# High weights meet high and low activations in one 512-column matmul

## The chip, the cores and the metric

One core of a Trainium2 chip runs the whole computation in one launch. The metric is the device time of that launch in microseconds (us). Before the change it is 994.75 us, the median of three runs from 994.37 to 995.06.

## The reference

The computation is one transformer layer followed by a second block of two, on 256 tokens of width 1024, all in float32. Only the matrix products and what follows them matter here:

```python
# first block
p = rmsnorm(x, g_attn) @ w_in                     # then two gated convolutions and stick-breaking attention
x = x + mixed @ w_out
x = x + square(relu(rmsnorm(x, g_ffn) @ w_ff1)) @ w_ff2
# second block, layer 0: retention; layer 1: differential attention over shared K and V
q, k, v, g = split(rms_norm(x, g) @ a_w_in)       # q and k are then rotated (cos, sin)
h = (silu(g) * rms_norm(retention(q, k, v))) @ a_w_out
kv = rms_norm(x, kv_norm) @ w_kv;  q = rms_norm(x, g) @ b_w_q
# after each of them
h = rms_norm(x, g) @ w_up                         # 2 x 2816 columns
hc = conv_b + sum(shift(h, 2 - j) * conv_w[j] for j in range(3))
h = (silu(hc[gate half]) * hc[up half]) @ w_down
```

## The kernel before

Every float32 operand of a large product is split in two parts that TensorE takes in its faster float32 form: high = the rounded value, low = the value minus high. A product is then three matmuls, high x high, high x low and low x high, added up in one PSUM bank. Weights come from memory packed in units of 128x1024 values; `loader` fetches two units at a time, `splitter` (`split_one`, L369) makes the high part on ScalarE (a copy) and the low part on VectorE (a subtraction) into a ring of eight units.

A unit is used in one of three ways. In `xstat_mm` and `down_mm` the activations are stationary and the weights move past them, 512 columns at a time. In `wstat` (L508) the weights are stationary: a unit is eight tiles of 128x128 and 256 tokens move past each, so that the result has channels on partitions and tokens along the row. For each of the eight tiles (a k step) it issues the three matmuls, 24 in a block, each of 256 columns, and `yield`s between steps. There are 142 such blocks: 14 in the mixing stage, 24 in the feed-forward stage (`ff_phase`), 16 in retention (`ret_phase`, four per head), 36 in each of the two convolution stages (`conv_phase`, a gate block and an up block per step) and 16 in the differential attention (`diff_phase`, two per head). The result of a block is 256 columns, half a bank; in retention and in the convolution stages two blocks share one bank.

The activations are held by `Acts` (L239): a high tile and a low tile of 8 x 256 values per partition, each allocated on its own. `sx` serves all stages, `sb` the queries of the differential attention.

What follows a block: `evac` of `ff_phase` (ScalarE relu out of the bank, VectorE square, `split_to`, which makes the high and low part for the down product); `rotate` (two VectorE products of the bank with cosine and sine, then a difference and a sum); `gate` (two `conv`s, each one ScalarE operation and two on VectorE that read the bank, then silu, a product and `split_to`); `evac` of `diff_phase` (one ScalarE copy).

The down products run behind the up blocks: `lagged` puts the down step of unit i five steps after its up step. `Down` holds four PSUM banks as accumulators (two for each half of the tokens). For the last seven units (TAIL) it does the first half of the tokens first, then hands that half to the chain of norms that leads to the next stage, and does the second half meanwhile.

The order of all instructions is fixed when the kernel is built, by a small simulation (`Flow`): each engine has a queue ordered by priority (CHAIN, ATT, EVAC, SPLIT, IDLE, MAIN), each operation has a cost in ns, and `Slots` stand for buffers: a process that asks for more than is free waits in line. `banks` are the eight PSUM banks, `cvs` three pairs of convolution buffers, `rots` one set of rotation buffers. On the chip each engine works off its list in that order and waits for semaphores. Every operation is recorded with the line L198, where the simulation issues it, so groups are told apart by the names of tiles: `hi`, `lo` are weights, `xh`, `xl` activations, `fh`, `fl` the inputs of a down product, `cv` convolution results.

Of the kernel before, what the change touches and what calls it, by code (L numbers as in the profile page):

```python
# [18 lines left out]
P = 128  # L19
# [219 lines left out]
class Acts:  # L239


    def __init__(self, hi, lo):
        self.hi, self.lo = hi, lo
        self.reset()

    def reset(self):
# [11 lines left out]
def chain_kernel(ctx: ExitStack, tc: tile.TileContext, x_in, wpack, gains, chan, small_rows, consts, out):  # L258
# [151 lines left out]
    mhalf = cpool.tile([P, 4], F32, tag="mhalf", name="mhalf")  # L410
    nc.gpsimd.memset(mhalf, -0.5)
    ch = cpool.tile([P, NCH], F32, tag="ch", name="ch")
    sx = Acts(cpool.tile([P, KD, S], F32R, tag="xh", name="xh"), cpool.tile([P, KD, S], F32R, tag="xl", name="xl"))

    junk = cpool.tile([P, 512], BF16, tag="junk", name="junk")

# [68 lines left out]
    def residual_post(t, acc, ready, g, hg):  # L485
# [19 lines left out]
        banks.put(2)  # L505
        return [stt(p, x, h, r, x, ALU.mult, ALU.add) for x, h in zip(xs, hs)]

    def wstat(dst, w, sx):  # L508
        hi, lo = yield from take("ws", w)
        h3 = hi.rearrange("p (k c) -> p k c", k=KD)  # L510
        l3 = lo.rearrange("p (k c) -> p k c", k=KD)
        for k in range(KD):
            if k % 4 == 0:
                yield sx.ready[0][k // 4]
                yield sx.ready[1][k // 4]
            o = pe(MAIN, 358, [
                mm(dst, h3[:, k, :], sx.hi[:, k, :], k == 0, False),
                mm(dst, h3[:, k, :], sx.lo[:, k, :], False, False),
                mm(dst, l3[:, k, :], sx.hi[:, k, :], False, k == KD - 1)])
            yield o.end  # L520
        release(ring, o)
        return o
# [377 lines left out]
    def ff_phase(fp):  # L900
        w1, w2 = "w_ff1", "w_ff2"
        fhs = slots(fp, TAIL + 2, [P, S], F32R, "fh")
        fls = slots(fp, TAIL + 2, [P, S], F32R, "fl")
        rls = slots(fp, 2, [P, S], F32, "rl")
        both = Slots(flow, TAIL + 2, lambda: (fhs.make(), fls.make()))
        ys = {}
        f8 = [fp.tile([P, 8, S], F32R, tag=f"f8{c}", name=f"f8{c}") for c in "hl"]
        nat = fp.tile([P, 2, D], F32, tag="nat", name="nat")
        r8 = [[Ev(), Ev()], [Ev(), Ev()]]

        def nat_evac_of(c):
            cs = slice(c * 512, c * 512 + 512)
            ks = slice(4 * c, 4 * c + 4)

            def nat_evac(t, d, o):
                yield o
                n = nat[:, t, cs]
                yield act(EVAC, n, d, AF.Relu)
                banks.put()
                yield tt(EVAC, n, n, n, ALU.mult)  # L920
                pt = yield from banks.get()
                yield tp(EVAC, [(pt[:, j * P:(j + 1) * P], n[:, j * P:(j + 1) * P]) for j in range(4)])
                tsl = slice(t * P, (t + 1) * P)
                yield from split_to(EVAC, f8[0][:, ks, tsl], f8[1][:, ks, tsl], pt.rearrange("p (k c) -> p k c", k=4))
                banks.put()
                flow.fire(r8[c][t])
            return nat_evac

        yield from xstat_tokens(w1, sx, [nat_evac_of(0), nat_evac_of(1)])
        for i in range(8):  # L930
            ys[i] = ((f8[0][:, i, :], f8[1][:, i, :]), flow.spawn(both_of(r8[i // 4])), None)

        def evac(pp, o, y):
            yield o
            rl = yield from rls.get()
            yield act(EVAC, rl, pp[:, :S], AF.Relu)
            banks.put()
            yield tt(EVAC, rl, rl, rl, ALU.mult)
            yield from split_to(EVAC, y[0], y[1], rl)
            rls.put()  # L940

        preload(AF.Silu)
        g_final = yield from load_gain(G_FINAL)
        a_pre = yield from load_gain(A_PRE)

        def chain(t, acc, o):
            xs = yield from big.get()
            ops = yield from residual_add(t, acc, o)
            r = yield from rstd_halves(CHAIN + 0.1 * t, halves(x_t[t]), ops)
            g, gop = g_final  # L950
            yield gop
            ops = [stt(CHAIN + 0.1 * t, xh_, xh_, r, g_, ALU.mult, ALU.mult) for xh_, g_ in zip(halves(x_t[t]), halves(g))]
            yield from prenorm(t, xs, [(a_pre, sx)], ops)
            big.put(3 if t == 1 else 1)

        dn = Down(w2, NF, chain, sx)
        for what, i in lagged(NF, 8):
            if what == "up":
                pp = yield from banks.get()
                o = yield from wstat(pp[:, :S], w1, sx)  # L960
                y = yield from both.get()
                ys[i] = (y, flow.spawn(evac(pp, o, y)), both)
            else:
                yield from dn.step(*ys.pop(i))
# [8 lines left out]
    def ret_phase(rp):  # L973
# [7 lines left out]
        o_ready = [[Ev(), Ev()] for _ in range(RH)]  # L981
        vs = Slots(flow, 1, lambda: [rp.tile([P, 2, 512], F32R, tag=f"v{c}", name=nm("v")) for c in "hl"])
        qs = [Slots(flow, 1, lambda w=w: rp.tile([P, 2, S], F32, tag=f"q{w}", name=nm("q"))) for w in range(2)]
        rots = Slots(flow, 1, lambda: [rp.tile([P, 2, S], F32, tag=f"rot{c}", name=nm("rot")) for c in "cs"])
        pds = Slots(flow, 1, lambda: [rp.tile([P, 384], d, tag=f"pd{c}", name=nm("pd")) for c, d in (("f", F32), ("h", F32R), ("l", F32R))])
        sgs = slots(rp, 2, [P, 512], F32, "sgl")

        def rotate(pp, o, dst):
            yield o
            for c in cops:  # L990
                yield c
            tcos, tsin = yield from rots.get()
            p3 = pp.rearrange("p (a c) -> p a c", a=2)
            a = tt(EVAC, tcos, p3, cosb.broadcast_to([P, 2, S]), ALU.mult)
            b = tt(EVAC, tsin, p3, sinb.broadcast_to([P, 2, S]), ALU.mult)
            yield a
            yield b
            banks.put()
            a = tt(EVAC, dst[:, 0, :], tcos[:, 0, :], tsin[:, 1, :], ALU.subtract)
            b = tt(EVAC, dst[:, 1, :], tsin[:, 0, :], tcos[:, 1, :], ALU.add)  # L1000
            yield a
            yield b
            rots.put()
# [60 lines left out]
        for h in range(RH):  # L1064
# [28 lines left out]
                f_pre = yield from load_gain(F0_PRE)  # L1093
            pr = []
            for what in range(2):
                pp = yield from banks.get()
                yield from wstat(pp[:, 0:S], "a_w_in_2", sx)
                o = yield from wstat(pp[:, S:2 * S], "a_w_in_2", sx)
                d = yield from qs[what].get()
                pr.append((d, flow.spawn(rotate(pp, o, d))))  # L1100
            pd_ev = flow.spawn(scores(h, pr[0][0], pr[1][0], pr[0][1], pr[1][1], box, dec, dop))
# [10 lines left out]
    def conv_phase(layer, fp, gain_ids, chain_of):  # L1112
# [2 lines left out]
        fls = slots(fp, TAIL + 2, [P, S], F32R, "fl")  # L1115
        both = Slots(flow, TAIL + 2, lambda: (fhs.make(), fls.make()))
        cvs = Slots(flow, 3, lambda: [fp.tile([P, S], F32, tag=f"cv{c}", name=nm("cv"), bufs=3) for c in range(2)])
        nat = fp.tile([P, 2, D], F32, tag="nat", name="nat")
        n_ready = [[Ev(), Ev()], [Ev(), Ev()]]

# [6 lines left out]

        def gate(pp, o_g, o_u, i, y, nat_i):
            cg, cu = yield from cvs.get()
            ps_g, ps_u = pp[:, 0:S], pp[:, S:2 * S]  # L1130
            if nat_i is not None:
                for e in n_ready[0] + n_ready[1]:
                    yield e
                o_g, o_u = [tp(EVAC, [(d[:, t * P:(t + 1) * P], nat[:, t, c0 + nat_i * P:c0 + (nat_i + 1) * P]) for t in range(2)])
                            for d, c0 in ((ps_g, 0), (ps_u, 512))]
            yield o_g
            yield o_u
            a = flow.spawn(conv(EVAC, ps_g, cg, 0, i))
            b = flow.spawn(conv(EVAC, ps_u, cu, 1, i))
            yield a  # L1140
            o = act(EVAC, cg, cg, AF.Silu)
            yield b
            banks.put()
            yield o
            yield tt(EVAC, cg, cg, cu, ALU.mult)
            yield from split_to(EVAC, y[0], y[1], cg)
# [23 lines left out]
            ys[i] = (y, flow.spawn(early(i, y)), both)  # L1170
        for what, i in lagged(NF2, 4):
            if what == "up":
                pp = yield from banks.get()
                o_g = yield from wstat(pp[:, 0:S], w_up, sx)
                o_u = yield from wstat(pp[:, S:2 * S], w_up, sx)
                y = yield from both.get()
                ys[i] = (y, flow.spawn(gate(pp, o_g, o_u, i, y, None)), both)
            else:
                yield from dn.step(*ys.pop(i))

    def diff_phase(dp, sb):
# [24 lines left out]
        aas = slots(dp, 2, [P, 384], F32, "aT")  # L1206
        o1s = slots(dp, 2, [P, 2, P], F32, "o1")

        def evac(pp, o, d, p):
            yield o  # L1210
            yield act(p, d, pp[:, :S], AF.Copy)
            banks.put()

        def head(h, p, q, k, qr, kr, v, v_in):
# [100 lines left out]
        for h in range(DH):  # L1315
            pr = []
            p = CHAIN + 0.5 if h >= DH - URGENT else ATT
            for what in range(2):
                pp = yield from banks.get()
                o = yield from wstat(pp[:, :S], "w_kv_2" if what == 0 else "b_w_q_2", sx if what == 0 else sb)  # L1320
                d = yield from qks[what].get()
                pr.append((d, flow.spawn(evac(pp, o, d, p if h >= DH - URGENT else EVAC))))
            heads.append(flow.spawn(head(h, p, pr[1][0], pr[0][0], pr[1][1], pr[0][1], v, v_in)))

        def coarse():
# [17 lines left out]
    def main():  # L1343
# [4 lines left out]
        with tc.tile_pool(name="retp", bufs=1, reuse_waits="tile") as rp:  # L1348
            yield from ret_phase(rp)
        with tc.tile_pool(name="bresp", bufs=1, reuse_waits="tile") as bp:  # L1350
            sb = Acts(bp.tile([P, KD, S], F32R, tag="bh", name="bh"), bp.tile([P, KD, S], F32R, tag="bl", name="bl"))
            with tc.tile_pool(name="cf0p", bufs=1, reuse_waits="tile") as fp:
                yield from conv_phase(0, fp, (F0_POST, KV_G, B_PRE), lambda f_post, kv_g, b_pre: (
                    lambda t, acc, o: chain_post(t, acc, o, f_post, [(kv_g, sx), (b_pre, sb)])))
# [103 lines left out]
```

## Time and profile before

| | |
|---|---|
| median of three runs | 994.75 us |
| profiled execution | 995.56 us |
| its span (first to last instruction) | 993.8 us |
| TensorE (PE) busy | 980.7 us, 99% |
| weight loads (PEld) busy | 876.1 us, 88% |
| VectorE (DVE) busy | 689.3 us, 69% |
| ScalarE (ACT) busy | 562.5 us, 57% |
| GpSimd (POOL) busy | 30.2 us, 3% |
| read from memory | 178.08 MB |

The span is what the profile sees of the execution; 1.76 us lie around it. Busy is the union of the times in which at least one instruction of the engine was under way. Matmuls overlap each other, and their ends are modelled, so for PE one reads the starts. A time in a row of the timeline is counted from the start of the span.

### The profile page before, as it was taken

How to read it: one execution, taken by the hardware profiler on the slowest of the kernel's cores; microseconds unless marked ns; L12 is line 12 of the kernel's file. 1: busy time of each engine (PE TensorE's matmuls, PEld its weight loads, DVE VectorE, ACT ScalarE, POOL GpSimd, SP SyncE). 2: the span in 40 equal slices, each digit the busy share in tenths (PEclk: the TensorE clock that was granted, in tenths of full speed). 3: DMA queues.
4: the chain of work that ended last, by engine and by line, in shares of the span. 5: the costliest groups of instructions: out<-in, count | busy, mean ns of one | idle time of the engine just before them, and what ended most of it. 6: DMA issues, size and time to landing. Idle time of an engine off the chain costs nothing.

```text
span 993.8 us, 15342 instructions
## 1 busy us (share of the span) xinstructions
PE 980.7 (99%) x6108; PEld 876.1 (88%) x6108; DVE 689.3 (69%) x1076; ACT 562.5 (57%) x952; POOL 30.2 (3%) x52
## 2 busy tenths in 40 slices
PE   7999999999999999999999999999999999999997
PEld 5899889999988989988889999997899789999996
DVE  5899775555558756665579666668777579776663
ACT  6654564444446444544567555556677767555551
POOL 1000000000000000000000000001000100000000
PEclk9999999999999999999999999999999999999999
DMA  8744455555436744554366555543733155655531
GB/s 300 257 133 176 179 212 187 195 173 207 171 128 228 264 164 147 178 188 174 123 219 250 185 192 173 209 169 135 266 148 134 54 199 205 236 182 177 184 107 43
DMA packets 28585, 180.14 MB, mean 181 GB/s; under 512 B 3168, under 2 KB 4448, under 8 KB 8672
## 3 DMA queue, kind: packets, MB, share of 16 engines
q1 hardware_dynamic: 28512, 179.14, 50.7%
q8 instruction: 48, 0.79, 0.3%
q14 instruction: 25, 0.20, 0.1%
HBM read 178.08 MB, written 1.05 MB: 180 GB/s over the span
## 4 chain that ended last, share of the span: by engine, by line
PE 92%; DVE 2%; ACT 2%; issue 2%; DMA 1%; POOL 1%; SPq 0%; DVEq 0%; POOLq 0%; ACTq 0%
PE bank L198 92%; ACT junk L198 1%; DVE lo L198 1%; DMA big<-gains 1%; POOL tiny L198 1%; DVE x L198 1%; DVE big L198 0%; ACT hi L198 0%; ACT L198 0%; DVE tiny L198 0%; ACT pe L198 0%; ACT aT L198 0%; DVE xl L198 0%; ACT dyh L198 0%; SPq L198 0%
## 5 line engine op out<-in xcount | busy, mean ns | idle before, releaser
L198 DVE TENSOR_TENSOR lo<-raw,hi 128x1024 fp32r<-128x1024 f32 (+1 forms) x344 | 393.7, 1153 | 129.7 <-ACT hi L198 128.5
L198 ACT ACTIVATE hi<-raw 128x1024 fp32r<-128x1024 f32 (+1 forms) x344 | 341.2, 1003 | 154.6 <-PE bank L198 138.9
L198 PE MATMUL bank<-xh,hi 128*128 128x256 f32 x1072 | 306.1, 286 | 0.0
L198 PE MATMUL bank<-xh,lo 128*128 128x256 f32 x1072 | 303.3, 283 | 0.0
L198 PE MATMUL bank<-xl,hi 128*128 128x256 f32 x1072 | 303.3, 283 | 0.0
L198 PEld LDWEIGHTS bank<-xh,hi 128*128 128x128 f32 x1072 | 205.4, 192 | 3.7 <-issue 1.0
L198 PEld LDWEIGHTS bank<-xl,hi 128*128 128x128 f32 x1072 | 205.4, 192 | 2.6
L198 PEld LDWEIGHTS bank<-xh,lo 128*128 128x128 f32 x1072 | 205.3, 191 | 0.0
L198 PE MATMUL bank<-hi,xh 128*128 128x512 f32 x288 | 114.1, 396 | 0.0
L198 PE MATMUL bank<-lo,xh 128*128 128x512 f32 x288 | 112.4, 390 | 0.2 <-DVE lo L198 0.2
L198 PE MATMUL bank<-hi,xl 128*128 128x512 f32 x288 | 112.5, 391 | 0.0
L198 DVE SCALAR_TENSOR_TENSOR cv<-bank,ch,cv 128x254 f32<-128x254 f32 (+1 forms) x176 | 72.5, 476 | 51.6 <-ACT cv L198 51.4
L198 PE MATMUL bank<-hi,fh 128*128 128x512 f32 x272 | 106.9, 393 | 0.0
L198 PE MATMUL bank<-lo,fh 128*128 128x512 f32 x272 | 106.5, 391 | 0.0
L198 PE MATMUL bank<-hi,fl 128*128 128x512 f32 x272 | 105.8, 389 | 0.0
L198 ACT ACTIVATE cv<-bank,ch 128x256 f32<-128x256 f32 x88 | 44.1, 561 | 61.4 <-PE bank L198 61.4
L198 PEld LDWEIGHTS bank<-hi,xl 128*128 128x128 f32 x288 | 54.0, 188 | 11.8 <-DVE xl L198 0.2
L198 PEld LDWEIGHTS bank<-lo,xh 128*128 128x128 f32 x288 | 54.2, 188 | 11.5 <-DVE lo L198 1.0
L198 PEld LDWEIGHTS bank<-hi,xh 128*128 128x128 f32 x288 | 54.1, 188 | 10.4
L198 PEld LDWEIGHTS bank<-hi,fl 128*128 128x128 f32 x272 | 51.1, 188 | 11.0
L198 PEld LDWEIGHTS bank<-hi,fh 128*128 128x128 f32 x272 | 51.3, 189 | 9.1
L198 PEld LDWEIGHTS bank<-lo,fh 128*128 128x128 f32 x272 | 51.3, 189 | 8.5
(167 smaller groups left out, 1039.8 us busy)
## 6 DMA issues: line engine op xcount, KB each, us to landing
raw<-wpack SPq DMA_DIRECT2D x155, 1024.0 KB, 4.8
big<-gains SPq DMA_DIRECT2D x12, 512.0 KB, 6.9
raw<-wpack SPq DMA_DIRECT2D x12, 512.0 KB, 6.9
x<-x SPq DMA_DIRECT2D x4, 256.0 KB, 6.1
out_dram<-x SPq DMA_DIRECT2D x4, 256.0 KB, 2.2
dec<-consts SPq DMA_DIRECT2D x4, 192.0 KB, 5.0
one<-consts SPq DMA_DIRECT2D x1, 384.0 KB, 6.3
ch<-chan SPq DMA_DIRECT2D x1, 213.5 KB, 5.9
```

The source lines that it names most:

```text
L198: fn(*a, **k)
```

## The change

In 124 of the 142 weight-stationary blocks the high weights meet high and low activations in one matmul. For that the two parts of the activations stand in one tile, and the moving operand of the first matmul is the view `both[:, :, k, :]`, two strips of 256 columns. Its result is 512 columns, a whole bank: high x high in the first half, high x low in the second. The low weights meet the high activations in a second matmul of 256 columns, which is added to the second half. After the block the two halves are added: `join` copies the second half out of the bank on ScalarE and adds the first on VectorE. The mixing stage and heads 6 and 7 of the differential attention keep three matmuls. Retention and the convolution stages take two banks per pair of blocks in place of one, and `gate` and `rotate` read the joined sums from new buffers (`sums`, two pairs; a third buffer in `rots`). The planner's cost of a k step is 352 (merged) and 360 (not merged), where it was 358.

```diff
 class Acts:
-    def __init__(self, hi, lo):
-        self.hi, self.lo = hi, lo
+    def __init__(self, both):
+        self.both = both
+        self.hi, self.lo = both[:, 0], both[:, 1]
         self.reset()
...
-    sx = Acts(cpool.tile([P, KD, S], F32R, tag="xh", name="xh"), cpool.tile([P, KD, S], F32R, tag="xl", name="xl"))
+    sx = Acts(cpool.tile([P, 2, KD, S], F32R, tag="xhl", name="xhl"))
...
+    def join(p, out, d):
+        yield act(p, out, d[:, S:], AF.Copy)
+        yield tt(p, out, d[:, :S], out, ALU.add)
+
     def wstat(dst, w, sx):
...
+        merged = dst.shape[-1] == 2 * S
         for k in range(KD):
...
-            o = pe(MAIN, 358, [
-                mm(dst, h3[:, k, :], sx.hi[:, k, :], k == 0, False),
-                mm(dst, h3[:, k, :], sx.lo[:, k, :], False, False),
-                mm(dst, l3[:, k, :], sx.hi[:, k, :], False, k == KD - 1)])
+            if merged:
+                o = pe(MAIN, 352, [
+                    mm(dst.rearrange("p (a c) -> p a c", a=2), h3[:, k, :], sx.both[:, :, k, :], k == 0, False),
+                    mm(dst[:, S:], l3[:, k, :], sx.hi[:, k, :], False, k == KD - 1)])
+            else:
+                o = pe(MAIN, 360, [
+                    mm(dst, h3[:, k, :], sx.hi[:, k, :], k == 0, False),
+                    mm(dst, h3[:, k, :], sx.lo[:, k, :], False, False),
+                    mm(dst, l3[:, k, :], sx.hi[:, k, :], False, k == KD - 1)])
...
         def evac(pp, o, y):                       # feed-forward
             yield o
             rl = yield from rls.get()
-            yield act(EVAC, rl, pp[:, :S], AF.Relu)
+            yield from join(EVAC, rl, pp)
             banks.put()
-            yield tt(EVAC, rl, rl, rl, ALU.mult)
+            yield stt(EVAC, rl, rl, 0.0, rl, ALU.max, ALU.mult)
...
-            tcos, tsin = yield from rots.get()
-            p3 = pp.rearrange("p (a c) -> p a c", a=2)
+            tcos, tsin, p3 = yield from rots.get()
+            for j in [flow.spawn(join(EVAC, p3[:, n, :], pp[n])) for n in range(2)]:
+                yield j
+            banks.put(2)
...
-                pp = yield from banks.get()
-                yield from wstat(pp[:, 0:S], "a_w_in_2", sx)
-                o = yield from wstat(pp[:, S:2 * S], "a_w_in_2", sx)
+                pp = yield from banks.get(2)
+                yield from wstat(pp[0], "a_w_in_2", sx)
+                o = yield from wstat(pp[1], "a_w_in_2", sx)
...
+        sums = Slots(flow, 2, lambda: [fp.tile([P, S], F32, tag=f"sum{c}", name=nm("sum"), bufs=2) for c in range(2)])
...
         def gate(pp, o_g, o_u, i, y, nat_i):
             cg, cu = yield from cvs.get()
...
+            else:
+                ps_g, ps_u = yield from sums.get()
+                yield o_g
+                yield from join(EVAC, ps_g, pp[0])
+                banks.put()
+                yield o_u
+                yield from join(EVAC, ps_u, pp[1])
+                banks.put()
...
-                pp = yield from banks.get()
-                o_g = yield from wstat(pp[:, 0:S], w_up, sx)
-                o_u = yield from wstat(pp[:, S:2 * S], w_up, sx)
+                pp = yield from banks.get(2)
+                o_g = yield from wstat(pp[0], w_up, sx)
+                o_u = yield from wstat(pp[1], w_up, sx)
...
+                merged = h < DH - 2
+                o = yield from wstat(pp if merged else pp[:, :S], "w_kv_2" if what == 0 else "b_w_q_2", sx if what == 0 else sb)
```

## Rows read from the trace of the kernel before

**Rows 1.** The page, its first part: engines' busy us, share of span, instructions.
```profile
PE 980.7 (99%) x6108; PEld 876.1 (88%) x6108; DVE 689.3 (69%) x1076; ACT 562.5 (57%) x952; POOL 30.2 (3%) x52
```

**Rows 2.** The page's chain of work that ended last, shares of the span.
```profile
PE 92%; DVE 2%; ACT 2%; issue 2%; DMA 1%; POOL 1%; SPq 0%; DVEq 0%; POOLq 0%; ACTq 0%
```

**Rows 3.** The view of waits, PE alone: total us, times, longest.
```profile
PE bank L198 <- DVE big L198: 3.2, 3, 2.6
...
```

**Rows 4.** Timeline of PE, 149.6 to 157.3 us: start, us, what.
```profile
149.64 0.39 PE L198 MATMUL bank<-hi,f8h 128*128 128x512 f32 x1
...
154.40 0.28 PE L198 MATMUL bank<-xh,hi 128*128 128x256 f32 x1
...
154.63 0.28 PE L198 MATMUL bank<-xh,lo 128*128 128x256 f32 x1
...
157.27 0.40 PE L198 MATMUL bank<-hi,f8h 128*128 128x512 f32 x1
```

**Rows 5.** Groups by form, PE: count, busy us, mean ns, idle before.
```profile
L198 PE MATMUL bank<-xh,hi 128*128 128x256 f32 x1072 | 306.1, 286 | 0.0
...
L198 PE MATMUL bank<-bh,hi 128*128 128x256 f32 x64 | 18.3, 286 | 0.0
```

**Rows 6.** Groups by form and timeline of PE, the mask matmul.
```profile
L198 PE MATMUL bank<-trib,identb 128*128 128x256 bf16 x8 | 1.6, 278 | 0.0
...
42.83 0.39 PE L198 MATMUL bank<-trib,identb 128*128 128x256 bf16 x2
```

**Rows 7.** Groups by form of ACT and of DVE.
```profile
L198 ACT ACTIVATE q<-bank 128x256 f32<-128x256 f32 x16 | 6.3, 395 | 5.4 <-PE bank L198 5.4
L198 ACT ACTIVATE junk<-x 128x512 bf16<-128x512 f32 x28 | 17.6, 629 | 16.9 <-DVE x L198 14.8 <-DMA x<-x 1.6
L198 ACT ACTIVATE junk<-bank 128x512 bf16<-128x512 f32 x24 | 14.3, 596 | 26.4 <-PE bank L198 25.9
...
L198 DVE TENSOR_TENSOR bank<-bank,tri 128x256 f32<-128x256 f32 x16 | 6.8, 425 | 2.1 <-PE bank L198 2.0
...
L198 DVE SCALAR_TENSOR_TENSOR cb<-gpad,ch,cb 128x256 f32<-128x256 f32 x60 | 25.5, 474 | 0.0
L198 DVE SCALAR_TENSOR_TENSOR cv<-bank,ch,cv 128x255 f32<-128x255 f32 x88 | 38.5, 478 | 51.6 <-ACT cv L198 51.4
```

**Rows 8.** Windows: us, busy us of PE, PEld, DVE, ACT, POOL; clock; DMA.
```profile
202.50:259.00 56.50, 56.50 (x363) 51.53 (x362) 32.13 (x40) 27.26 (x42) 0.00 (x0) 1.00 0.53 189
...
567.50:652.50 85.00, 85.00 (x602) 80.09 (x602) 58.17 (x91) 48.41 (x71) 0.00 (x0) 1.00 0.53 186
...
709.40:771.20 61.80, 61.55 (x507) 57.27 (x507) 44.68 (x113) 46.08 (x138) 4.15 (x6) 1.00 0.49 181
```

**Rows 9.** Windows of 5 us, start of the first convolution stage.
```profile
522.50:527.50 5.00, 5.00 (x44) 5.00 (x44) 5.00 (x13) 3.41 (x7) 0.00 (x0) 1.00 1.03 432
...
537.50:542.50 5.00, 5.00 (x33) 4.51 (x32) 5.00 (x9) 2.66 (x7) 0.00 (x0) 1.00 0.60 218
```

**Rows 10.** Timeline of DVE and of PE at that start.
```profile
520.44 4.13 DVE L198 SCALAR_TENSOR_TENSOR cv<-bank,ch,cv 128x255 f32<-128x255 f32 x10
...
527.06 0.42 DVE L198 TENSOR_TENSOR fl<-cv,fh 128x256 fp32r<-128x256 f32 x1
...
530.67 3.99 DVE L198 SCALAR_TENSOR_TENSOR cv<-bank,ch,cv 128x255 f32<-128x255 f32 x10
...
533.32 0.28 PE L198 MATMUL bank<-xh,hi 128*128 128x256 f32 x1
```

**Rows 11.** Timeline of ACT, DVE and PE, end of the first convolution stage.
```profile
665.41 1.02 ACT L198 ACTIVATE cv<-bank,ch 128x256 f32<-128x256 f32 x2 [1.57 <-PE bank L198]
...
668.03 1.22 DVE L198 TENSOR_TENSOR lo<-raw,hi 128x1024 fp32r<-128x1024 f32 x1
...
670.07 0.42 DVE L198 TENSOR_TENSOR fl<-cv,fh 128x256 fp32r<-128x256 f32 x1 [0.48 <-ACT fh L198]
...
672.49 0.39 PE L198 MATMUL bank<-hi,fl 128*128 128x512 f32 x1
```

More of the change, by code (lines that the diff above doesn't have):

```diff
@@ L959, in ff_phase @@
                 pp = yield from banks.get()
-                o = yield from wstat(pp[:, :S], w1, sx)
+                o = yield from wstat(pp, w1, sx)
                 y = yield from both.get()
@@ L983, in ret_phase @@
         qs = [Slots(flow, 1, lambda w=w: rp.tile([P, 2, S], F32, tag=f"q{w}", name=nm("q"))) for w in range(2)]
-        rots = Slots(flow, 1, lambda: [rp.tile([P, 2, S], F32, tag=f"rot{c}", name=nm("rot")) for c in "cs"])
+        rots = Slots(flow, 1, lambda: [rp.tile([P, 2, S], F32, tag=f"rot{c}", name=nm("rot")) for c in "csq"])
         pds = Slots(flow, 1, lambda: [rp.tile([P, 384], d, tag=f"pd{c}", name=nm("pd")) for c, d in (("f", F32), ("h", F32R), ("l", F32R))])
@@ L997, in rotate @@
             yield b
-            banks.put()
             a = tt(EVAC, dst[:, 0, :], tcos[:, 0, :], tsin[:, 1, :], ALU.subtract)
@@ L1129, in gate @@
             cg, cu = yield from cvs.get()
-            ps_g, ps_u = pp[:, 0:S], pp[:, S:2 * S]
             if nat_i is not None:
+                ps_g, ps_u = pp[:, 0:S], pp[:, S:2 * S]
                 for e in n_ready[0] + n_ready[1]:
@@ L1135, in gate @@
                             for d, c0 in ((ps_g, 0), (ps_u, 512))]
-            yield o_g
-            yield o_u
+                yield o_g
+                yield o_u
+            else:
+                ps_g, ps_u = yield from sums.get()
+                yield o_g
+                yield from join(EVAC, ps_g, pp[0])
+                banks.put()
+                yield o_u
+                yield from join(EVAC, ps_u, pp[1])
+                banks.put()
             a = flow.spawn(conv(EVAC, ps_g, cg, 0, i))
@@ L1142, in gate @@
             yield b
-            banks.put()
+            if nat_i is not None:
+                banks.put()
+            else:
+                sums.put()
             yield o
@@ L1207, in diff_phase, with evac @@
         o1s = slots(dp, 2, [P, 2, P], F32, "o1")
-        def evac(pp, o, d, p):
+        def evac(pp, o, d, p, merged):
             yield o
-            yield act(p, d, pp[:, :S], AF.Copy)
+            if merged:
+                yield from join(p, d, pp)
+            else:
+                yield act(p, d, pp[:, :S], AF.Copy)
             banks.put()
@@ L1319, in diff_phase @@
                 pp = yield from banks.get()
-                o = yield from wstat(pp[:, :S], "w_kv_2" if what == 0 else "b_w_q_2", sx if what == 0 else sb)
+                merged = h < DH - 2
+                o = yield from wstat(pp if merged else pp[:, :S], "w_kv_2" if what == 0 else "b_w_q_2", sx if what == 0 else sb)
                 d = yield from qks[what].get()
-                pr.append((d, flow.spawn(evac(pp, o, d, p if h >= DH - URGENT else EVAC))))
+                pr.append((d, flow.spawn(evac(pp, o, d, p if h >= DH - URGENT else EVAC, merged))))
             heads.append(flow.spawn(head(h, p, pr[1][0], pr[0][0], pr[1][1], pr[0][1], v, v_in)))
@@ L1350, in main @@
         with tc.tile_pool(name="bresp", bufs=1, reuse_waits="tile") as bp:
-            sb = Acts(bp.tile([P, KD, S], F32R, tag="bh", name="bh"), bp.tile([P, KD, S], F32R, tag="bl", name="bl"))
+            sb = Acts(bp.tile([P, 2, KD, S], F32R, tag="bhl", name="bhl"))
             with tc.tile_pool(name="cf0p", bufs=1, reuse_waits="tile") as fp:
```

## Prediction

> **What bounds the kernel now.** Read the page's first part: TensorE (PE) is busy 99% of a span of 993.8 us, its weight loads 88%, VectorE (DVE) 69%, ScalarE (ACT) 57% [rows 1]. A busy matmul row says little, since matmuls overlap, so look next at the chain that ended last: 92% of it is PE writing PSUM banks [rows 2]. Then the view of waits, for PE alone: six rows, the longest 3.2 us in all [rows 3]. So PE hardly ever stands still, and what counts is how far apart its matmuls start, not how long each is drawn. The timeline gives that. In [rows 4] the 21 matmuls of 512 columns from 149.64 to 154.40 start (154.40 - 149.64) / 21 = 226.7 ns apart; then one weight-stationary block, 24 matmuls of 256 columns, goes from 154.40 to 157.27, 119.6 ns each. Both hold at a granted clock of 1.00, which is the level of 2.4 GHz [rows 8]. At one column a cycle 512 columns are 213.3 ns and 256 are 106.7 ns: the same 13 ns is left over on each, whatever its width. That excess per matmul is what the change can save; the columns stay as they are.
>
> **The merged matmuls.** In a k step three starts of 119.6 ns (358.8 ns) become one of 226.7 and one of 119.6 (346.3 ns): 12.5 ns less. 24 blocks of the feed-forward stage, 16 of retention, 72 of the two convolution stages and 12 of the attention stage are merged, 124 of the 142 behind the 1072 + 64 rows of a kind in [rows 5] (142 x 8 = 1136). 124 x 8 = 992 steps x 12.5 ns = 12.4 us, all on the engine that sets the end.
> What no row shows is a 512-column matmul whose moving operand is two strips of 256 columns, 8 KB apart. Bounds: 226.7 ns if strips cost nothing; 2 x 119.6 = 239.2 ns if each strip pays what a matmul of its own pays, which leaves no gain; and, if a change of strip paid a second excess of 13 ns on top, 252 ns, a loss of 12.7 us. The nearest row is the mask matmul of the mixing stage, whose moving operand is also two strips (a [2, 128] view): two of them take 0.39 us where one takes 0.278, so they start 0.11 us apart, no more than a matmul of 256 columns in one piece [rows 6]. I take 226.7. The new planner costs in the diff, 352 against 360, would be 8 ns instead of 12.5; I keep them as a rival below.
> One rule speaks against the size of this. The Trainium skill (TensorE: Matmul & The Clock Gate, "Wait — 56ns, not 53.3ns?") puts the fixed cost of a warm matmul at 2.5 ns. By that, estimated from the page, two starts of 109.2 ns become one of 215.8 ns, and the sum is 992 x 2.5 ns = 2.5 us. The trace does not agree: 119.6 and 226.7 ns, with a weight load in front of every matmul.
>
> **The joins.** Each merged block ends with two half sums in one bank, which ACT copies and DVE adds. A 256-element ACT copy out of a bank is 395 ns, a DVE add with one operand in a bank 425 ns [rows 7]. DVE gets 124 x 0.425 = 52.7 us, and the feed-forward square, as max-and-multiply, goes from 425 to about 474 ns (+1.2 us over 24). ACT gets a copy in 72 + 16 blocks (34.8 us); in the feed-forward and attention blocks it takes the place of an evacuation that was there. The convolutions and the rotation then read SBUF where they read a bank: on DVE that is 474 against 478 ns, nothing; on ACT 629 against 596 for 512 elements, so some 33 ns x 72 = 2.4 us. DVE comes to 689 + 54 = 743 us, ACT to 600 us: neither becomes the bound as a whole.
> By stage [rows 8]: in a steady convolution stretch of 85 us (ten iterations) DVE does 58.2 us and gets 20 joins, 8.5: 66.7 of some 83 us. ACT: 48.4 + 20 x 0.42 = 56.8. Feed-forward, 56.5 us with ten blocks: DVE 32.1 + 4.7. Attention, 61.8 us: DVE 44.7 + 12 x 0.425 = 49.8. There is room everywhere, the work stands beside PE, and the next use of what a join makes is several blocks off. I cost the joins in the steady stretches at nothing. What covers them is that slack; were it gone, 0.8 us would fall on PE per block.
>
> **Where the cover is thin.** (a) The start of each convolution stage. DVE is busy 5.00 of 5.00 us there from 522.5 to 542.5 [rows 9]: three gates are worked off from 520.44 and the next three from 530.67 [rows 10]. An up step now takes two banks at its start, while the four accumulators hold four of eight. The gates of the first two merged up steps wait for one of three cv pairs, free when an early gate ends (its last write at 527.06, [rows 10]), and only then join and let their banks go. The first frees its two about two copies and two adds later: 527.5 + 2 x (0.40 + 0.43) plus queueing behind a split, 1.2 us, is some 530.5 us. The second starts at about 529.6 and frees its first bank near 532. The third merged up step, which PE starts at 533.32, needs two banks, the first down steps four. This just fits; a queue longer by one DVE batch would cost up to 2 us. I take 0.4 us each time, 0.8 for the two stages.
> (b) The end of each convolution stage. The last gate begins with the ACT row at 665.41 and ends with the DVE row at 670.07 (0.42 long); PE reads its output at 672.49 [rows 11]. Slack 2.0 us. The join puts 0.40 + 0.43 + a handoff of 0.1 in front, 0.9 us, and with a weight split between them (1.2 us in the row at 668.03) 2.1. I take 0.1 us each.
> (c) The last two heads keep their old evacuation, and their chain starts earlier by the 12 merged blocks, as PE does. Nothing.
> (d) Weight supply: loading and splitting do not change; the ring of eight units is refilled during the block, and PE asks 1.3% faster for it while DMA stands at 0.53 of its time [rows 8]. Nothing; if splits ran late it would be DVE's 8.5 us per stretch that did it, and there 16 us remain.
> (e) The single tile for high and low activations, in place of two, adds no instruction; nothing, with a split's 1.2 us per stage as the upper end should a write wait for the other half.
>
> **Sum.** 993.8 - 12.4 + 0.8 + 0.2 = 982.4 us span; around it lie 995.56 - 993.8 = 1.76 us, so the profiled execution would be 984.2. It was 0.8 us above the median of the runs shown (994.75), which puts the median at 983.4 us, -1.1%.
>
> **Rivals.**
> 1. *Strips cost some.* If the merged matmul starts 232 ns apart instead of 226.7 (what 352 in the diff would mean, 352 - 120), the gain is 7 ns x 992 = 7 us: 994.75 - 7 + 1 = 988.8. For it: no f32 row with two strips, and two numbers in the diff. Against: [rows 6]. 14%.
> 2. *Banks.* At the start of a convolution stage up steps four to six stand in line for banks until whole gates end. The second batch in [rows 10] has its last convolution end at about 534.6 plus the new joins, six of 0.43 us on a full DVE, 537.2, against 533.3 when PE wants the banks: 4 us, and 3 us more in the steps after, while the line drains; x 2 stages is near 7 us lost after a true gain of 12.4: about 989.4. For it: DVE's full 20 us. Against: a gate now gives its bank up after the join, not after its convolutions. 10%.
> 3. *The excess belongs to something that stays.* If it were paid per change of weight tile and not per matmul, high to low and back are still two changes per step, and only the difference between two equal-weight starts would go, 2.5 ns or so: 992 x 2.5 = 2.5 us, 994.75 - 2.5 + 1 = 993.3, no change. Against: the first two starts of the block, from high to high to low weights, take 0.23 us, the other 22 take 2.64, 0.12 each [rows 4]. The fixed cost in the page's rule above would come to the same. 5%.
> 4. *Slower.* Place: the 992 merged matmuls. Mechanism: the jump between strips stalls the stream. Price: 0.99 us per ns; from 238.2 ns on (12.5 ns less the 1 us of waits) the kernel is slower; at 252 ns it takes 994.75 + 12.7 + 1 = 1008.4. Against it [rows 6], whose strips are short, bf16 and repeat the same data, so not the same case. 9%.
>
> **How the numbers follow.** The forecast has 62%; its own range is 981 (no waits, and 120 in place of 119.6 ns: 992 x 13.3 = 13.2 us, 981.6) to 986 (3 us of waits on top). Rivals 1 and 2 reach to 991; 3 and 4 lie outside, 14%. So the range is 981 to 991 us. A measurement of this kernel can tell 0.2%, 2 us. Faster: 62 + 14 + 10 = 86%; the same: rival 3, 5%; slower: rival 4, 9%.
>
> **What would show it.** In the timeline of the changed kernel: starts of 227 and 120 ns in turn in a merged block and 2.77 us from block to block, in place of 2.87; one kind of matmul of 512 columns, 992 times, and weight loads fewer by 992. DVE near 743 us busy, ACT near 600. PE's waits still a few us, new ones only near 533, 838, 672 and 977 us, less what was saved by then. Wrong: a spacing of 232 or more, PE waits for banks in every up step, or DVE full beyond the starts of the convolution stages.

## The result, and the profile after

The changed kernel takes 986.58 us (median of 5 runs, 986.30 to 987.54) against 994.70 (5 runs): a ratio of 0.992, 95% interval 0.9909 to 0.9932, 8.1 us less. The forecast was 983.4 in a range of 981 to 991.

The page of the changed kernel, its first part, answers to [rows 1]; below it one group by form, the merged matmul, and the two groups of what a join adds in a convolution stage:

```profile
PE 973.0 (99%) x5116; PEld 821.2 (83%) x5116; DVE 736.2 (75%) x1200; ACT 587.7 (60%) x1040; POOL 31.0 (3%) x52
...
L198 PE MATMUL bank<-xhl,hi 128*128 128x512 f32 x944 | 338.0, 399 | 0.0
L198 DVE TENSOR_TENSOR sum<-bank,sum 128x256 f32<-128x256 f32 x72 | 30.0, 418 | 0.0
L198 ACT ACTIVATE sum<-bank 128x256 f32<-128x256 f32 x72 | 26.2, 367 | 0.0
```

992 matmuls and as many weight loads are gone; 944 merged ones stand in the row shown and 48 in that of the attention's second activation tile. DVE has grown by 47 us, ACT by 25, and PE is at 99% as before. Its waits answer to [rows 3], eight rows now; the first three:

```profile
PE bank L198 <- POOL warm L419: 1.5, 1, 1.5
PE bank L198 <- DVE big L198: 0.8, 2, 0.6
PE bank L198 <- DVE lo L198: 0.8, 3, 0.3
```

None of the eight is for a bank or for the buffer that a join fills. Most of the wait for `big` lies in the first 16.5 us, before any merged block; it was 3.2 us in all in the profile of before and between 0.8 and 3.0 in those that follow. It differs from execution to execution, and with it the start of the work. So compare the traces from the first weight-stationary matmul to the last matmul of all, before and then after:

```profile
27.61 0.28 PE L198 MATMUL bank<-xh,hi 128*128 128x256 f32 x1
...
987.23 0.39 PE L198 MATMUL bank<-hi,fl 128*128 128x512 f32 x1
...
25.77 0.28 PE L198 MATMUL bank<-xhl,hi 128*128 128x256 f32 x1
...
977.76 0.39 PE L198 MATMUL bank<-hi,fl 128*128 128x512 f32 x1
```

That is 959.6 and 952.0 us: 7.6 us less, where the spans differ by 9.3 and the medians by 8.1. The first block starts at 25.8 to 27.8 us in the nine profiles of this document, so medians of a few runs can be off by some tenths of a us, up to about one; below, this stretch of each trace stands beside the median.

So the gain must be in the starts of the matmuls. The timeline of PE in the first convolution stage, where [rows 4] stood for the kernel before:

```profile
571.42 0.39 PE L198 MATMUL bank<-xhl,hi 128*128 128x512 f32 x1
571.64 0.28 PE L198 MATMUL bank<-xhl,lo 128*128 128x256 f32 x1
571.76 0.40 PE L198 MATMUL bank<-xhl,hi 128*128 128x512 f32 x1
571.99 0.28 PE L198 MATMUL bank<-xhl,lo 128*128 128x256 f32 x1
572.11 0.40 PE L198 MATMUL bank<-xhl,hi 128*128 128x512 f32 x1
572.35 0.28 PE L198 MATMUL bank<-xhl,lo 128*128 128x256 f32 x1
...
575.29 0.40 PE L198 MATMUL bank<-xhl,hi 128*128 128x512 f32 x1
...
577.06 0.40 PE L198 MATMUL bank<-hi,fh 128*128 128x512 f32 x1
```

Only the first step of the pair of blocks is as forecast: 571.42, 571.64, 571.76, that is 0.34 us. From 572.11 to 575.29 nine steps take 3.18 us, 353.3 ns each, not 346.3; the wide start is followed by the narrow one after 0.24 us, not 0.227. Both blocks take 577.06 - 571.42 = 5.64 us.

The windows of the same work as in [rows 8] (feed-forward, ten convolution iterations), and the same columns:

```profile
198.40:254.00 55.60, 55.60 (x280) 46.71 (x280) 36.21 (x50) 28.01 (x40) 0.00 (x0) 1.00 0.54 189
...
563.30:647.10 83.80, 83.80 (x441) 71.47 (x440) 65.97 (x110) 53.14 (x91) 0.00 (x0) 1.00 0.53 188
```

DVE does 65.97 us of 83.8 in ten iterations (66.7 were forecast), 36.21 in the feed-forward stretch (36.8). The stretch of 85.0 us has become 83.8, at the same clock of 1.00.

### The profile page after: what moved, and what is told of

It reads as the page before. It is cut to its first block, busy times and chain, and to the rows that moved or that the text cites. A ratio compares the mean times of both kernels' runs of the same rounds, so it can differ in the third digit from the quotient of the medians.

```text
span 984.5 us, 13622 instructions
## 1 busy us (share of the span) xinstructions
PE 973.0 (99%) x5116; PEld 821.2 (83%) x5116; DVE 736.2 (75%) x1200; ACT 587.7 (60%) x1040; POOL 31.0 (3%) x52
## 4 chain that ended last, share of the span: by engine, by line
PE 92%; DVE 3%; ACT 2%; issue 2%; DMA 1%; POOL 1%; SPq 0%; DVEq 0%; POOLq 0%; ACTq 0%
PE bank L198 92%; DVE lo L198 1%; ACT junk L198 1%; DMA raw<-wpack 1%; POOL tiny L198 1%; DVE x L198 1%; ACT hi L198 1%; DVE big L198 0%; ACT L198 0%; DVE xhl L198 0%; DVE tiny L198 0%; ACT pe L198 0%; DVE nat L198 0%; SPq L198 0%; ACT dyh L198 0%
## 5 line engine op out<-in xcount | busy, mean ns | idle before, releaser
L198 PE MATMUL bank<-xhl,hi 128*128 128x512 f32 (+1 forms) x1200 | 386.2, 375 | 0.0
L198 PE MATMUL bank<-xhl,lo 128*128 128x256 f32 x1072 | 301.0, 281 | 0.0
L198 PEld LDWEIGHTS bank<-xhl,hi 128*128 128x128 f32 x1200 | 217.3, 189 | 42.6 <-issue 0.3
L198 PEld LDWEIGHTS bank<-xhl,lo 128*128 128x128 f32 x1072 | 202.7, 189 | 2.5
L198 PE MATMUL bank<-hi,xhl 128*128 128x512 f32 x576 | 185.1, 394 | 0.3 <-ACT xhl L198 0.2
L198 PEld LDWEIGHTS bank<-hi,xhl 128*128 128x128 f32 x576 | 108.0, 188 | 23.2 <-ACT xhl L198 0.7
L198 PE MATMUL bank<-lo,xhl 128*128 128x512 f32 x288 | 112.5, 391 | 0.8 <-DVE lo L198 0.8
L198 PEld LDWEIGHTS bank<-lo,xhl 128*128 128x128 f32 x288 | 54.1, 188 | 12.4 <-DVE lo L198 1.9
L198 DVE SCALAR_TENSOR_TENSOR cv<-sum,ch,cv 128x255 f32<-128x255 f32 (+1 forms) x144 | 60.6, 478 | 1.0 <-ACT cv L198 1.0
L198 ACT ACTIVATE cv<-sum,ch 128x256 f32<-128x256 f32 x72 | 39.3, 588 | 2.7 <-DVE sum L198 2.6
```

The costliest lines, as they stand in the source:

```text
L198: fn(*a, **k)
```

## Experiments

The forecast's mechanism was there and half of its size was not: 6.7 ns a step (360.0 in the middle of a block before, 353.3 now) x 992 = 6.6 us, where 12.4 stood. Four theories for the missing ns: A, the jump between the two strips of the moving operand; B, the alternation of 512-column and 256-column matmuls; C, the second matmul adding to the half that the first has just written; and that the joins took it. The runs below (4 to 11 of each kernel) were timed beside the kernel before, which stood at 994.67 us in the first four and 994.80 in the last three.

**Strips side by side.** High and low activations of one k are neighbours, so the moving operand is one piece:

```diff
-        self.hi, self.lo = both[:, 0], both[:, 1]
+        self.hi, self.lo = both[:, :, 0], both[:, :, 1]
-    sx = Acts(cpool.tile([P, 2, KD, S], F32R, tag="xhl", name="xhl"))      # sb alike
+    sx = Acts(cpool.tile([P, KD, 2, S], F32R, tag="xhl", name="xhl"))
-    ... sx.both[:, :, k, :] ...
+    ... sx.both[:, k] ...
```

> The merged k step takes 353 ns in the trace where 346.3 were forecast: starts of 236.8 and 116.6 ns. Here high and low activations of one k stand side by side, so that the moving operand is one piece of 512 columns; nothing else changes. Theory A (the jump between the two strips costs): starts fall to 227 and 120, a step to 347, and 992 x 6 ns = 6 us go: about 980.5. Theory B (the alternation of a 512-column and a 256-column matmul costs, whatever the operand looks like) and theory C (the second matmul adds to the half that the first has just written): step stays at 353, time within 1 us of 986.6.

Measured: 987.52 us, ratio 0.9927 (0.9915 to 0.9939), as the changed kernel; the stretch of the trace is 952.0 us, the same as there. Six steps of its timeline, the first and the last row:

```profile
572.98 0.40 PE L198 MATMUL bank<-xhl,hi 128*128 128x512 f32 x1
...
575.10 0.40 PE L198 MATMUL bank<-xhl,hi 128*128 128x512 f32 x1
```

2.12 us, 353.3 ns each, the same. Theory A falls: two strips 8 KB apart cost nothing.

**Joins without merging.** All of the change, with each merged matmul taken apart again:

```diff
-                    mm(dst.rearrange("p (a c) -> p a c", a=2), h3[:, k, :], sx.both[:, :, k, :], k == 0, False),
+                    mm(dst[:, :S], h3[:, k, :], sx.hi[:, k, :], k == 0, False),
+                    mm(dst[:, S:], h3[:, k, :], sx.lo[:, k, :], False, False),
```

(The planner's cost of the step is 360 here.)

> The changed kernel with its joins, its banks and its single activation tile, but each merged matmul taken apart again into two of 256 columns, one for each half of the bank. The forecast costs the joins and the bank handling at 1 us in all: then this stands at 994.7 + 1 = 995.7, within 1.5 us, and the merging alone is worth the whole difference to 986.6. If the joins and the wait for banks cost several us (what the rival on banks says), it stands at 998 or above, and merging is worth more than the k steps show (992 x 6.7 = 6.6 us). If it is below 994, something beside the matmuls was gained.

Measured: 994.24 us, ratio 0.9995 (0.9986 to 1.0004). 124 joins, the second banks and the single tile cost nothing that can be measured; the forecast had 1.0 us for them. Merging alone is then the ratio of 0.992 to 0.9995, 7.5 us; by the traces (959.0 us here, 952.0 with merging) it is 7.0. Its windows, of the attention's eight heads and of ten convolution iterations:

```profile
708.90:769.80 60.90, 60.89 (x507) 57.08 (x506) 48.81 (x125) 45.80 (x138) 4.16 (x6) 1.00 0.51 184
559.00:644.00 85.00, 85.00 (x602) 80.09 (x602) 66.33 (x110) 53.17 (x91) 0.00 (x0) 1.00 0.53 186
```

DVE does 66.33 us in the 85.0 where it did 58.17 [rows 8], and PE starts the same 602 matmuls in it: eight more us beside PE, at no cost. The whole stage, from its first block to the first of the next stage, takes 191.8 us in both. In the attention the heads take 60.9 us where they took 61.8, without a matmul fewer. The joins bring another order of the instructions there; that this order gained the 0.9 us is likely but not shown.

**All wide matmuls first.** In a block the eight of 512 columns, then the eight of 256:

```diff
         for k in range(KD):
...
-                o = pe(MAIN, 352, [
-                    mm(dst.rearrange("p (a c) -> p a c", a=2), h3[:, k, :], sx.both[:, :, k, :], k == 0, False),
-                    mm(dst[:, S:], l3[:, k, :], sx.hi[:, k, :], False, k == KD - 1)])
+                o = pe(MAIN, 232, [mm(dst.rearrange("p (a c) -> p a c", a=2), h3[:, k, :], sx.both[:, :, k, :], k == 0, False)])
...
+        for k in range(KD if merged else 0):
+            o = pe(MAIN, 120, [mm(dst[:, S:], l3[:, k, :], sx.hi[:, k, :], False, k == KD - 1)])
+            yield o.end
```

> In a merged block first the eight 512-column matmuls, then the eight of 256 columns; same instructions, operands and banks. Theory B (each change from 256 to 512 columns costs): one change of width per block in place of eight, starts of 227 in the first run of eight but for the first few, 120 in the second; 8 steps fall from 2.83 us to about 2.79, and 124 x 0.04 = 4 to 5 us go: about 982. Theory A (strips): the 512-column starts stay at 236, time within 1 us of 986.6. Theory C (adding to the half just written): starts fall too, as in theory B; the next kernel tells the two apart.

Measured: 982.75 us, ratio 0.988 (0.9865 to 0.9895), the best version here, 3.8 us below the change by the medians and 4.6 by the traces (947.4 us). The timeline of PE over two blocks, after a down step of 512-column matmuls and before the next:

```profile
570.57 1.98 PE L198 MATMUL bank<-xhl,hi 128*128 128x512 f32 x8
572.38 1.11 PE L198 MATMUL bank<-xhl,lo 128*128 128x256 f32 x8
573.33 2.00 PE L198 MATMUL bank<-xhl,hi 128*128 128x512 f32 x8
575.17 1.12 PE L198 MATMUL bank<-xhl,lo 128*128 128x256 f32 x8
576.13 0.40 PE L198 MATMUL bank<-hi,fh 128*128 128x512 f32 x1
```

Read the differences of the starts. Eight wide ones that follow wide ones take 572.38 - 570.57 = 1.81 us, 226 ns each. The eight that follow narrow ones take 1.84: the first of them are late, 30 ns together. The narrow ones take 0.95 and 0.96, 119 and 120 each. Both blocks: 5.56 us, against 5.64 alternating. That is theory B, or C.

**The other half.** The narrow matmul adds to the half written 256 columns earlier:

```diff
-                    mm(dst[:, S:], l3[:, k, :], sx.hi[:, k, :], False, k == KD - 1)])
+                    mm(dst[:, :S], l3[:, k, :], sx.hi[:, k, :], False, k == KD - 1)])
```

> The 256-column matmul adds to the first half of the bank (written 256 columns earlier) in place of the second, which the 512-column matmul has written last. The sum of the halves is the same. Theory C (the addition comes too soon after the write): step falls from 353 to 347 ns, about 980.5 us. Theories A and B: step stays at 353, time within 1 us of 986.6.

Measured: 987.46 us, ratio 0.9927 (0.9915 to 0.994), as the changed kernel; the trace has 951.9 us, and 353.3 ns a step. Theory C falls. That agrees with the kernel before, where each matmul of a block adds to what the last one wrote and they start 120.0 ns apart. Of the four theories B is left.

**Four and four.** On the grouped order, the narrow matmuls in two runs of four:

```diff
+            for j in range(k - 3, k + 1) if merged and k % 4 == 3 else ():
+                o = pe(MAIN, 120, [mm(dst[:, S:], l3[:, j, :], sx.hi[:, j, :], False, j == KD - 1)])
+                yield o.end
```

> The dose of theory B: in a merged block four matmuls of 512 columns, four of 256, and the same again, two changes from narrow to wide per block (eight in the changed kernel, one with all eight in a row, at 986.6 and 982.75 us). In the traces the first five wide starts after a narrow run are late by 6.6, 9.0, 1.7, 6.0 and 4.1 ns, and the first two narrow ones early by 6.7 and 0.8: a change and back costs some 20 ns once a run is long. Theory B: one more change per block, 124 x 18 ns (four wide starts, not five, fall in the first run) = 2.2 us above 982.75, about 985. If only the pairing of one wide and one narrow matmul in a step cost (theory B2), two changes would cost as little as one: 983, within 0.6.

Measured: 985.37 us, ratio 0.9906 (0.9893 to 0.992). Theory B2 falls. Eight changes from narrow to wide per block take 986.58 us, two 985.37, one 982.75; by the traces 952.0, 949.9 and 947.4. Changes between long runs are dear and those between short ones cheap: the second change costs 2.6 us (124 x 21 ns), by the medians and by the traces alike, and the six more of the changed kernel together only 1.2 by the medians and 2.1 by the traces.

**All heads.** On the grouped order, `merged = True` in place of `h < DH - 2`.

> All eight heads of the attention merged, on top of the grouped order (982.75 us). The forecast took it that the last heads' evacuation lies on the path: PE waits 0.6 us for the last head's output in every trace so far. Theory P (the path): the four blocks are worth 4 x 0.09 = 0.35 us to PE, the join puts 0.9 us in front of the last head, on the path: slower by 0.5 to 0.9 us, 983.3 to 983.7. Theory H (hidden): 0.35 us faster, 982.4.

Measured: 984.34 us, ratio 0.9899 (0.9883 to 0.9914), 1.6 us slower than the grouped order (2.4 by the traces); theory P, and more than it said. The timeline of PE at the end of the stage, and a window of 7 us behind it, first here and then in the grouped kernel:

```profile
774.75 0.40 PE L198 MATMUL bank<-hi,dyl 128*128 128x512 f32 x1
776.34 0.58 PE L198 MATMUL bank<-ident,o 128*128 128x128 f32 x2 [1.20 <-ACT o L198]
777.49 0.60 PE L198 MATMUL bank<-hi,dyh 128*128 128x512 f32 x1 [0.56 <-ACT dyh L198]
...
778.32 0.63 PE L198 MATMUL bank<-hi,dyl 128*128 128x512 f32 x1
778.74 0.63 PE L198 MATMUL bank<-hi,dyh 128*128 128x512 f32 x1
...
778.00:785.00 7.00, 7.00 (x26) 5.60 (x25) 4.12 (x7) 4.90 (x12) 0.55 (x1) 0.77 0.00 0
...
778.00:785.00 7.00, 7.00 (x32) 5.62 (x31) 4.95 (x10) 6.40 (x15) 1.07 (x2) 1.00 0.03 5
```

The second row is new: PE waits 1.20 us for the last head's normed output, as well as the 0.56 that every version has. It has nothing left to run while that chain ends. And behind the two waits the granted clock fell: 0.77 in the window, a mean of the levels of 1.2 and 2.4 GHz, where the grouped kernel, with the 0.56 us alone, has 1.00. The wide matmuls start 0.42 us apart there, and the nine starts behind 777.49 take 3.75 us, for 2.25 in the grouped kernel. The new wait and these 1.5 us, less the 0.35 that merging gives, are the 2.4 us.

**The mixing stage.** On the grouped order, its 14 blocks merged; `qk_evac` and `conv_a` join:

```diff
-            yield act(EVAC, dst, pp[:, :S], AF.Copy)
+            yield from join(EVAC, dst, pp)
...
-            yield act(EVAC, ac, pc[:, :S], AF.Copy)
+            yield from join(EVAC, ac, pc)
...
-            yield tt(EVAC, up[:, 2:], ph[:, :S], ac, ALU.mult)
+            yield from join(EVAC, sh, ph)
+            yield tt(EVAC, up[:, 2:], sh, ac, ALU.mult)
```

(The third block of `conv_a` likewise.)

> The 14 blocks of the mixing stage merged too, with joins, on top of the grouped order (982.75 us). Theory G: the stage is as much bound by PE as the others; 14 x (8 x 13.3 - 20) ns = 1.2 us go, 981.5. Theory V: DVE, which does the 31-tap convolution there, and the ScalarE copies are late for the down step; PE waits eat the gain: 982.75 to 985.

Measured: 989.10 us, ratio 0.9943 (0.993 to 0.9955), 6.3 us slower than the grouped order (7.4 by the traces); theory V, beyond its upper end. The windows (up to the last rows of the convolution, then the down product, then the part of it at the lower clock) and two rows of the timeline of PE:

```profile
33.90:97.00 63.10, 63.03 (x362) 53.29 (x362) 63.10 (x111) 33.82 (x61) 0.00 (x0) 1.00 0.50 177
91.20:121.30 30.10, 25.21 (x105) 19.98 (x104) 21.10 (x47) 12.25 (x23) 1.61 (x3) 0.89 0.22 77
...
102.50:109.30 6.80, 5.39 (x13) 4.28 (x14) 2.00 (x6) 0.75 (x2) 0.00 (x0) 0.50 0.00 0
...
100.69 0.97 PE L198 MATMUL bank<-ident,gpad 128*128 128x128 f32 x4 [2.46 <-DVE gpad L198]
103.91 0.80 PE L198 MATMUL bank<-hi,yh 128*128 128x512 f32 x1 [2.25 <-ACT yh L198]
```

DVE is busy 63.10 us of 63.10: here it is DVE, with the 31-tap convolution, that sets the end, and 14 joins of 0.42 us are 5.9 us more work in front of its last outputs. Counted from the stage's first block, the last low part for the down product (`yl` of the convolution) is written 7.4 us later than in the grouped kernel. PE stands still twice, 2.46 and 2.25 us, and during the second time the granted clock fell: it is 0.50, the level of 1.2 GHz, from 102.5 to 109.3 us, so that the matmuls behind the two idle times ran slower too. In the grouped kernel without it the same stretch had DVE at 57.35 of 57.60 us.

## Why the prediction was right, and where not

*What bounds the kernel* was right: PE's starts decide. Work put into DVE's spare time costs nothing, as the joins without merging show.

*The merged matmuls* is the step that was mis-sized: 6.6 us in steps of 353.3 ns, for 12.4 in steps of 346.3. I took each width's spacing from the inside of a long run and put the two together. A wide matmul behind a narrow one starts its successor late. The trace of before shows it in each down step that follows a block; the timeline of PE, the first down step of the first convolution stage, ends at the 533.32 of [rows 10]:

```profile
530.57 0.40 PE L198 MATMUL bank<-hi,fh 128*128 128x512 f32 x1
```

Twelve wide starts in 533.32 - 530.57 = 2.75 us are 229.2 ns each, not the 226.7 of [rows 4]: 30 ns for one change of width, paid over the first five starts. That row was at hand, and the changed kernel makes eight such changes in a block; with one wide matmul between two narrow ones each costs only some 6.6 ns (353.3 - 226.7 - 120.0).

That the time lies in the range at all is in part luck. The forecast's own range ended at 986, and only with 3 us of waits that did not come; the stretch up to 991 was there for rivals 1 and 2, and neither of their causes was found.

*Rival 1* had the size nearly right (232 ns, 988.8 us) for a wrong reason: strips cost nothing, as the mask matmul of [rows 6] had said. Rival 4 falls with it. Rival 3 falls: the merging is worth 7.0 to 7.5 us, not 2.5. Nor does the 2.5 ns of the Trainium skill's page (TensorE: Matmul & The Clock Gate, "Wait — 56ns, not 53.3ns?") fit the trace of any version here: 226 ns inside the grouped runs are 13 ns above the columns' 213.3.

*The joins* were costed right at nothing. DVE came to 736 us busy, not 743, and ACT to 588, not 600, though the work grew about as forecast: the durations of all rows add up to 749 us before and 804 after on DVE, 55 more, and to 617 and 651 on ACT, 34 more. Busy counts a time once, and instructions that follow each other at once overlap, as the add at 662.22 below and the row behind it do by 0.09 us. The rest is small: an add out of a bank took 418 ns for 425, and the max-and-multiply of the feed-forward stage 425 for 474.

*Where the cover is thin.* (a) No wait: PE starts the third merged up step right behind the last down matmul, and rival 2 falls:

```profile
529.20 0.40 PE L198 MATMUL bank<-hi,fl 128*128 128x512 f32 x1
529.44 0.40 PE L198 MATMUL bank<-xhl,hi 128*128 128x512 f32 x1
```

(Rival 2 also read the end of the second batch too early: in the trace of before two more convolution rows of it follow the row at 530.67, and end at 535.8, not 534.6.) (b) The rows at the end of the stage, for [rows 11]:

```profile
660.92 0.36 ACT L198 ACTIVATE sum<-bank 128x256 f32<-128x256 f32 x1
...
662.22 0.42 DVE L198 TENSOR_TENSOR sum<-bank,sum 128x256 f32<-128x256 f32 x1
662.55 0.47 DVE L198 SCALAR_TENSOR_TENSOR cv<-sum,ch,cv 128x255 f32<-128x255 f32 x1
...
665.64 0.43 DVE L198 TENSOR_TENSOR fl<-cv,fh 128x256 fp32r<-128x256 f32 x1 [0.49 <-ACT fh L198]
...
666.84 0.39 PE L198 MATMUL bank<-hi,fl 128*128 128x512 f32 x1
```

The join's add waits behind a weight split and a `fl`, so 1.3 us lie between copy and add; the slack of 2.0 us is 0.8. It held. (c) was right, and the run with all heads shows why: there the cover is gone.

*Sum.* The medians differ by 8.1 us, the traces behind the first block by 7.6, and of these 6.6 are the steps. The heads of the attention, 61.7 us before and 59.8 after (from the stage's first block to the first matmul of its output product), gained 1.9, of which the 96 steps explain 0.6; 0.9 came without merging too, and 0.4 I cannot place. The other stages together gained 5.9, for 6.0 of their steps. What makes a wide start late behind a narrow one was not found, only that neither the strips nor the written half have a part in it. The weight load in front of each matmul was in every version, so a part of it in this is neither shown nor excluded.

## What to carry to other kernels

Where matmuls follow each other without a pause, price a change by the distance of their starts, and read that distance for each sequence of widths that the new code will issue, the first starts behind a change included, not only inside long runs. If two widths must mix, issue them in long runs: the same instructions in another order gave 3.8 us more. And look stage by stage for the engine that is full before adding work beside PE: 0.42 us per block was free in five stages and cost 6.3 us in the one whose DVE had nothing left.

## What the runs showed of the hardware

Matmuls with a weight load each started 120.0 ns apart with 256 columns and 226.7 with 512 as long as the width stayed; alternating, a pair took 353.3, in a pattern that repeats every three pairs (in the means over the pairs of blocks of the first convolution stage, with the strips side by side, 232.6 and 117.4, 240.9 and 120.0, 235.7 and 113.3). After a run of narrow ones five wide starts were late, by 6.6, 9.0, 1.7, 6.0 and 4.0 ns in the grouped kernel. The pair took the same, within half a ns, with one strip or two, and with either half of the bank. The granted clock fell to its lower level behind idle times of PE of 2.46 and 2.25 us (0.50 in the window of 6.8 us), and behind 1.20 and 0.56 us (0.77 in one of 7); behind 0.56 us alone it stayed at 1.00.
